# Three changes of order in a hybrid encoder layer on one core: late sums, half weight tiles, hung loads

## The chip, the cores and the metric

The kernel runs on one NeuronCore of a Trainium2 chip. Its time is the device time in microseconds of one execution. Engines of the core: PE (matrix products), DVE and ACT (element-wise work, copies out of the accumulators), POOL (here mostly an issuer of DMAs, also those that add into their target) and SP (an issuer of DMAs). Each takes its instructions in order.

## The reference

One layer of an encoder is run on a prompt of 1024 frames and a sample of 32 frames, with shared weights, in float32:

```python
h = rms_norm(x, g_pre_mix)
qa, ka, va, ra, alr, qb, kb, vb, ga, gb = split_cols(h @ w_in)
oa, s_gla = gla_branch(qa, ka, va, ra, alr, w_a2, b_a2, g_gla, gla_s0, gla_block)   # 4 heads, gated linear recurrence
ob, k_rows, v_rows = attn_fn(qb, kb, vb, rel_bias)                                  # 8 heads, band of 9 chunks of 64
mix = (sigmoid(ga) * (oa @ w_br_a) + sigmoid(gb) * (ob @ w_br_b)) @ w_out
x = x + rms_norm(mix, g_post_mix)
f, conv_new = conv_ffn(rms_norm(x, g_pre_ffn), conv_s0, w_up, conv_w, conv_b, w_down)
x = x + rms_norm(f, g_post_ffn)
gate = sigmoid(rms_norm(x, g_pre_ple) @ w_ple_gate)
x = x + rms_norm(gate * (pe @ w_ple), g_post_ple)
```

The sample's attention reads cached keys and values as well (`cache_attn_k`, `cache_attn_v`), its recurrence starts from a given state (`state_gla`). The outputs are the new x of both groups, the last keys and values, the recurrence's states and the convolution's.

## The kernel before

Prompt and sample lie side by side, T = 1056 columns; a row is a tile of 128 features by 1056 columns, 528 KB. Products in float32 are made of three passes of a rounded format: every operand is split into a high part (a copy by ACT) and a low part (the difference, by DVE), and PE multiplies high by high, high by low and low by high. So each weight tile is loaded (`raw`, two buffers), split into `whi` and `wlo`, and used.

The order of PE, DVE and ACT is the order of the program text, written out by hand from stage to stage. The order of the DMAs on SP and POOL is planned at build time: the planner places each where it expects its operands and its buffer to be ready. On the chip an issuing engine then waits, in that order, at each DMA until its operands are there, with all later ones behind it.

**Band stage (about 303 to 576 us).** Eight heads (hp 0 to 3, hd 0 and 1) of nine blocks each: eight blocks of 128 queries and one for the sample. One loop runs over all 72 blocks. For block i it makes the scores (`probs`: PE products L1039 and L1040 into the only accumulator pair `two`, then L1045 on DVE, which adds the bias and takes the row minimum), then the transposes of block i-1 (`transposed`: PE L1052, ACT's high part L1054, DVE's low part L1055 put off into `LOWS`), ACT's exponential L1046, a step of the next head's preparation (`prepare`: splits of q, k and v, copies of kh and kl to the other 64 partitions by DMAs L1001 and L1004, transposes of v), one `piece` of a filler (the products L862 to L895 of other weight tiles, whose results `fv`, four buffers, ACT evacuates in L734 and L870), and at last the output of block i-2 (`third`: PE L1093; `gather`: ACT copies half of it in L1059, DVE adds the other half to it in L1060; L1117 to L1119 for the sample). The accumulators `one` are four banks, `mm` two, `two` one pair. Before the loop, rows q, k and v of the first two heads are loaded (L1242), 18 pieces run, and the steps of the first `prepare` lie between them. Their loads are kc (L965) and cv (L967), the cached keys and values, and the bias tile of each head (L979, then two POOL memsets L980 and L981).

**Recurrence stage (about 576 to 866 us).** Four heads of four segments, u = 0 to 15. In each, level factors of segment u+1 (`X`, DVE L1361 to L1398, ACT L1377 to L1383) are made beside the products of segment u; L1451 and L1454 turn the scores, L1522 uses them. The filler goes on: `load_tile` (L790 loads half a tile, L792 a whole one), ACT L817/L820 and DVE L818/L821 split it, POOL adds finished parts into DRAM (L749) and places new operands (L777, L778). In a head's last segment the sample's state tile `ss` (one buffer) is loaded (L1539), used, updated by L1528 and stored (L1529). `sr` rows are loaded in L1544 and stored in L1599.

**Branch stage (about 866 to 992 us).** 12 products of a band row block (`branch_b`), then 28 of the other branch (`branch_a`, L1968 to L1970, about 3 us each) in a hand-written sequence `seq`; `order_w` lists their 30 half tiles of weights in order of use. `weights_load` loads two halves into one tile of `raw`, `split_weights` splits half i two products before its use (ACT L1830, DVE L1831), and with every even i asks for the pair i+2. `pair_load` (L1937) loads gate rows into buffers that POOL's adding DMAs (L1952) must have left. After this stage come the output product, the feed-forward part and the embedding part, which the change does not touch.

Of the kernel before, what the change touches and what calls it, by code (L numbers as in the profile page):

```python
# [12 lines left out]
F32 = mybir.dt.float32  # L13
# [3 lines left out]
ALU = mybir.AluOpType  # L17

P = 128
D = 1024  # L20
KT = 8
NP = 1024
NS = 32
# [22 lines left out]
LATE = 4  # L46
# [68 lines left out]
def emit(tc, a):  # L115
# [12 lines left out]
    def tl(p, shape, dt=F32, tag=None, bufs=None):  # L128
        tag = tag or nm("t")
        kw = {} if bufs is None else {"bufs": bufs}  # L130
        return p.tile(list(shape), dt, name=nm(tag), tag=tag, **kw)
# [27 lines left out]
    wp = pool("wp")  # L159
# [802 lines left out]
    def band_loads(hp):  # L962
        d = B.setdefault(hp, {})
        d["kc"] = tl(bp, [P, 512], tag="kc")
        dma.dma_start(d["kc"], a["cache_k"][hp])  # L965
        d["cv"] = tl(bp, [P, 4, P], tag="cv")
        dma.dma_start(d["cv"], a["cache_v"][hp])  # L967

    def prepare(g):
        hp, hd = divmod(g, 2)  # L970
        d = B[hp]
        r = slice(64 * hd, 64 * hd + 64)
        o = slice(64 - 64 * hd, 128 - 64 * hd)
        if hd == 0:
            band_loads(hp)
        qs, kh, kl = [tl(bp, [P, w], F32R, tag=f"{x}{hd}") for x, w in (("qs", T), ("kh", T + 512), ("kl", T + 512))]
        vs = tl(bp, [P, 13, P], F32R, tag=f"vs{hd}")
        bias = tl(bp, [P, NS + 640], tag="bias", bufs=2)
        dma.dma_start(bias, a["rel"][2 * hp + hd])  # L979
        po.memset(bias[64:128, NS : NS + 64], NEG)  # L980
        po.memset(bias[0:64, NS + 576 : NS + 640], NEG)  # L981
        d[hd] = qs, kh, kl, vs, bias
        parts = [(slice(0, HT), d["k"][:, one]), (slice(HT, T), d["k"][:, two]), (slice(T, T + 512), d["kc"])]

        def high(i):
            ac.activation(kh[r, parts[i][0]], parts[i][1][r], AF.Copy)

        def low_part(i):
            ve.tensor_tensor(kl[r, parts[i][0]], parts[i][1][r], kh[r, parts[i][0]], op=ALU.subtract)

        high(0)
        yield
        high(1)
        low_part(0)
        yield
        high(2)
        low_part(1)
        yield
        ac.activation(qs[r], d["q"][r], AF.Copy)
        low_part(2)  # L1000
        dma.dma_start(kh[o].bitcast(F32), kh[r].bitcast(F32))  # L1001
        yield
        ve.tensor_tensor(qs[o, one], d["q"][r, one], qs[r, one], op=ALU.subtract)
        dma.dma_start(kl[o].bitcast(F32), kl[r].bitcast(F32))  # L1004
        yield
        ps = ps_one()
        for j in range(8):
            pe.transpose(ps[:, 64 * j : 64 * j + 64], d["v"][r, j * P : (j + 1) * P], ident[r, r])
        src = ps.rearrange("p (j f) -> p j f", f=64)
        ac.activation(vs[:, 0:8, r], src, AF.Copy)  # L1010
        ve.tensor_tensor(qs[o, two], d["q"][r, two], qs[r, two], op=ALU.subtract)
        ve.tensor_tensor(vs[:, 0:8, o], src, vs[:, 0:8, r], op=ALU.subtract)
        yield
        ps = ps_one()
        pe.transpose(ps[:NS, :64], d["v"][r, NP:], ident[r, r])
        ac.activation(vs[:NS, 12:13, r], ps[:NS, :64].rearrange("p (j f) -> p j f", f=64), AF.Copy)
        ve.tensor_tensor(vs[:NS, 12:13, o], ps[:NS, :64].rearrange("p (j f) -> p j f", f=64), vs[:NS, 12:13, r], op=ALU.subtract)
        ac.activation(vs[:, 8:12, r], d["cv"][:, :, r], AF.Copy)
        yield
        ve.tensor_tensor(vs[:, 8:12, o], d["cv"][:, :, r], vs[:, 8:12, r], op=ALU.subtract)  # L1020
        yield

    LOWS = []

    def band_head(hp, hd):
        r = slice(64 * hd, 64 * hd + 64)
# [30 lines left out]
        def gather(ps, n, out):  # L1057
            t = tl(bp, [P, 256], tag="ot", bufs=2)[r, :n]
            ac.activation(t, ps[o, :n], AF.Copy)  # L1059
            ve.tensor_tensor(out, ps[r, :n], t, op=ALU.add)  # L1060

        def pair(t):
            use = [range(max(0, 2 * t + j - 4), 2 * t + j + 1) for j in range(2)]
# [35 lines left out]
        def sample():  # L1099
            got = {}  # L1100

            def first():
                got["s"] = probs(NP, NS, NP, 512 + NS, -NS)

            def second():
                p = got["p"] = tl(bp, [P, 10, P], F32R, tag="pt", bufs=3)
                transposed([(got["s"], NS + b * P, P) for b in range(4)], NS, [p[:, :4, x : x + NS] for x in (0, NS)])
                transposed([(got["s"], 0, NS)], NS, [p[:NS, 4:5, x : x + NS] for x in (0, NS)])

            def third():  # L1110
                vs = d[hd][3]
                ps = ps_one()
                for k in range(5):
                    n = P if k < 4 else NS
                    pe.matmul(ps[:, : 2 * NS], vs[:n, 8 + k], got["p"][:n, k, : 2 * NS], start=(k == 0), stop=(k == 4))
                t = tl(bp, [P, 256], tag="ot", bufs=2)[r, : 2 * NS]
                ac.activation(t, ps[o, : 2 * NS], AF.Copy)  # L1117
                ve.tensor_tensor(t, ps[r, : 2 * NS], t, op=ALU.add)
                ve.tensor_tensor(d["ob"][r, NP:], t[:, :NS], t[:, NS:], op=ALU.add)  # L1119

            return [(first, second, third)]

# [138 lines left out]
    for i in range(len(WORK) + SK + 1):  # L1261
        g, j = divmod(i, NW)
        hp, hd = divmod(g, 2)
        if g < 8:
            if j == 0:
                if hd == 0:
                    band_sums(hp)
                steps = prepare(g + 1) if g < 7 else decays(0)
            if j == 3 and hd == 0:
                B[hp]["ob"] = evt()  # L1270
            WORK[i][0]()
            if SK <= i:
                WORK[i - SK][1]()
            B[hp]["exp"].pop()()
            next(steps, None)
            if j % 3 == 2:
                next(made, None)
            if hd == 0 and hp < 3 and j in (5, 7) or hd and hp < 3 and j == 0:
                band_row(hp + 1, {5: 0, 7: 1, 0: 2}[j])
            if g == 7 and j in (6, 7):  # L1280
                head_value(0, j - 6)
            if j == 5 and g:
                weight_sum(*divmod(g - 1, 4), B[hp]["sums"][hd][0:1, 0:1])
            if j % 3 == 1 and g:
                n = 3 * (g - 1) + j // 3
                if n < 4 * HK:
                    branch_sum(n, B[hp]["sums"][hd][0:1, 0:1])
        piece()
        n = i - SK - 1
        if n >= 0 and WORK[n][2]:  # L1290
            WORK[n][2]()
        if len(WORK) <= i < len(WORK) + SK:
            WORK[i - SK][1]()
        for f in LOWS:
            f()
        LOWS.clear()
        flush()
        if fill["n"] < 18 + (BAND_PIECES - 18) * (i + 1) / (len(WORK) + SK + 1):
            piece()
        next(end, None)  # L1300
        if n >= 0 and n % (2 * NW) == 2 * NW - 1:
            end = band_end(n // (2 * NW))
            next(end)
# [230 lines left out]
    def loads(u):  # L1534
        g, h, s, t0, nt = seg(u)
        r = R.setdefault(u, {})
        if nt > 256:
            r["ss"] = tl(gp, [P, 256], tag="ss")
            dma.dma_start(r["ss"], a["state_gla"][h])  # L1539

    def gates(u):
# [286 lines left out]
    def branch_half(key, t):  # L1828
        h, l = wsp[key] = [tl(wp, [P, HK, P], F32R, tag=x, bufs=4) for x in ("whi", "wlo")]
        ac.activation(h, t, AF.Copy)  # L1830
        ve.tensor_tensor(l, t, h, op=ALU.subtract)  # L1831
# [3 lines left out]
    def weight_of(n, m):  # L1835
        if n == "b":
            return a["w_br_b"][3, :, HK * (m % 2) : HK * (m % 2) + HK].rearrange("p k c -> p (k c)")
        if n[0] == "a":
            return branch_quarter(int(n[1]) - 1, int(n[2]) - 1, m)
        return d_wa[m, :, ("s0", "s1", "s3", "s2").index(n)]  # L1840

    def weights_load(i):
        if i < len(order_w) and order_w[i] not in raws:
            raw = tl(wp, [P, KT, P], tag="raw", bufs=2)
            for j, u in enumerate(order_w[i : i + 2]):
                raws[u] = raw[:, HK * j : HK * j + HK]
                dma.dma_start(raws[u].rearrange("p k c -> p (k c)"), weight_of(*u))

    for n in (4, 5, 6):
        dma.dma_start(gb[n] if n < 6 else oa[KT - 1][0].bitcast(F32), d_gb[n])  # L1850
# [181 lines left out]
        at.setdefault(use[u] - 2, []).append(u)  # L2032

    def split_weights(u):
        i = order_w.index(u)
        if i % 2 == 0:
            weights_load(i + 2)
        branch_half(u, raws.pop(u))

    weights_load(0)  # L2040
    work = {0: [(first_sum, 0), (first_split, 0)], 1: [(first_sum, 1), (first_split, 1)], 2: [(first_sum, 2), (first_split, 2)],
            3: [(first_sum, 3), (first_split, 3)], 4: [(t1_split, 0), (t1_split, 1)], 5: [(t1_split, 2), (t1_split, 3)], 6: [(t2_sum, 0), (t2_sum, 1)],
            7: [(t2_split, 0), (t2_sum, 2)], 8: [(t2_split, 1), (t2_sum, 3)], 9: [(t2_split, 2), (t2_split, 3)], 10: [(third_sum, 0)], 11: [(b22_split, 0)],
# [1264 lines left out]
```

## Time and profile before

| | us |
|---|---|
| median of 3 runs | 1864.64 |
| lowest, highest | 1861.52, 1873.78 |
| the profiled execution | 1872.21 |
| its span | 1870.5 |
| PE busy in it | 1826.9 |

The profile's numbers are of the profiled execution, its span a little shorter than its time. A row of the timeline gives start, duration, engine, line, operation, the tile written and those read, the shape, and in brackets the idle time of the engine before it and what ended that. A row of the waits gives total, times and longest. A row of a stretch of time gives its length, the busy time of PE, PEld (weight loads), DVE, ACT and POOL, then TensorE's mean granted clock (1.00 is full), the busy share of the DMA engines and GB/s. SPq is SP's queue of DMAs.

### The profile page before, as it was taken

The page shows a single profiled execution, that of the slowest core. Times are in us where ns is not written, and L with a number is a line of the kernel's source. Part 1 is how long each engine was busy: PE and PEld are TensorE (multiplying, and loading weights), DVE is VectorE, ACT ScalarE, POOL GpSimd, SP SyncE. Part 2 cuts the span into 40 slices and gives each one's busy share as a digit, 9 for nine tenths or more (in the row PEclk, how much of TensorE's full clock was granted, in tenths as well). Part 3 has the DMA queues.
Part 4 walks back from the last instruction along what each step waited for, and adds up shares of the span by engine and source line. Part 5 has one row for each costly group of instructions (what it writes and reads, how often), then busy time and mean ns, then how long its engine had stood idle before and what let it go on. Part 6 is the DMA issues. An engine that isn't in the chain of part 4 may idle for free.

```text
span 1870.5 us, 36262 instructions
## 1 busy us (share of the span) xinstructions
PE 1826.9 (98%) x14000; PEld 1789.8 (96%) x14000; DVE 1298.1 (69%) x2451; ACT 1005.0 (54%) x2126; POOL 351.9 (19%) x609
## 2 busy tenths in 40 slices
PE   8999999999999999999999999999999999999996
PEld 8999998899999998998999999999999999999996
DVE  6955542666656875877847776888888875568776
ACT  7544233666667776766636555433333345555555
POOL 0043441132201121110010121122223211000102
PEclk9999999999999999999999999999999999999998
DMA  7278986778667889877595477676878779887746
GB/s 284 84 223 244 273 220 204 193 209 244 193 176 240 263 258 226 225 182 269 190 250 174 159 266 279 198 229 211 243 210 224 177 216 307 294 267 250 237 136 111
DMA packets 171449, 413.24 MB, mean 221 GB/s; under 512 B 21956, under 2 KB 56972, under 8 KB 170380
## 3 DMA queue, kind: packets, MB, share of 16 engines
q1 hardware_dynamic: 116156, 252.99, 40.7%
q0 software_dynamic: 53680, 153.24, 32.5%
q10 hardware_dynamic: 1440, 4.69, 0.6%
q8 instruction: 110, 1.80, 0.4%
q14 instruction: 63, 0.52, 0.1%
HBM read 270.68 MB, written 181.97 MB: 242 GB/s over the span
## 4 chain that ended last, share of the span: by engine, by line
PE 82%; DMA 6%; DVE 5%; ACT 5%; issue 2%; POOL 0%; SPq 0%; ACTq 0%; DVEq 0%; POOLq 0%
PE two L2533 6%; PE two L2531 6%; PE two L2532 6%; PE mm L228 3%; PE mm L226 3%; PE mm L227 3%; PE two L2980 3%; PE two L2982 3%; PE two L2981 3%; PE two L641 3%; PE two L642 3%; PE two L643 3%; PE mm L893 3%; PE mm L862 3%; PE mm L863 2%; PE mm L895 2%
## 5 line engine op out<-in xcount | busy, mean ns | idle before, releaser
L2982 PE MATMUL two<-d,wlo 128*128 128x264 f32 x616 | 174.3, 283 | 0.8 <-DVE wlo L2716 0.8
L2981 PE MATMUL two<-d,whi 128*128 128x264 f32 x616 | 174.7, 284 | 0.2 <-DVE d L2667 0.2
L2980 PE MATMUL two<-d,whi 128*128 128x264 f32 x616 | 174.6, 284 | 0.0
L2521 ACT ACTIVATE whi<-ws 128x512 fp32r<-128x512 f32 x88 | 55.5, 632 | 161.8 <-PE two L2532 154.5
L862 PE MATMUL mm<-xh,whi 128*128 128x264 f32 x448 | 135.7, 303 | 2.2 <-ACT fv L870 2.1
L863 PE MATMUL mm<-xl,whi 128*128 128x264 f32 x448 | 128.0, 286 | 0.0
L864 PE MATMUL mm<-xh,wlo 128*128 128x264 f32 x448 | 127.6, 285 | 0.0
L2532 PE MATMUL two<-ml,whi 128*128 128x264 f32 x448 | 126.4, 283 | 0.0
L2533 PE MATMUL two<-mh,wlo 128*128 128x264 f32 x448 | 126.0, 284 | 0.0
L2531 PE MATMUL two<-mh,whi 128*128 128x264 f32 x448 | 125.8, 283 | 0.0
L2982 PEld LDWEIGHTS two<-d,wlo 128*128 128x128 f32 x616 | 116.4, 189 | 1.1 <-DVE wlo L2716 1.0
L2981 PEld LDWEIGHTS two<-d,whi 128*128 128x128 f32 x616 | 115.8, 188 | 0.4 <-DVE d L2667 0.4
L2980 PEld LDWEIGHTS two<-d,whi 128*128 128x128 f32 x616 | 115.7, 188 | 0.0
L893 PE MATMUL mm<-xh,whi 128*128 128x352 f32 x312 | 109.6, 351 | 3.4 <-ACT fv L734 3.4
L895 PE MATMUL mm<-xh,wlo 128*128 128x352 f32 x312 | 101.9, 327 | 0.0
L894 PE MATMUL mm<-xl,whi 128*128 128x352 f32 x312 | 101.7, 326 | 0.0
L642 PE MATMUL two<-tl,whi 128*128 128x264 f32 x320 | 90.7, 284 | 0.0
L641 PE MATMUL two<-th,whi 128*128 128x264 f32 x320 | 90.7, 283 | 0.0
L643 PE MATMUL two<-th,wlo 128*128 128x264 f32 x320 | 90.7, 284 | 0.0
L862 PEld LDWEIGHTS mm<-xh,whi 128*128 128x128 f32 x448 | 85.5, 191 | 4.2 <-ACT fv L870 3.5
L2716 DVE TENSOR_TENSOR wlo<-wraw,whi 128x512 fp32r<-128x512 f32 (+1 forms) x81 | 51.7, 644 | 50.9 <-ACT whi L2715 50.8
L863 PEld LDWEIGHTS mm<-xl,whi 128*128 128x128 f32 x448 | 85.1, 190 | 0.0
(802 smaller groups left out, 6854.3 us busy)
## 6 DMA issues: line engine op xcount, KB each, us to landing
raw<-in_w_in SPq DMA_DIRECT2D x36, 512.0 KB, 4.6
d_b<-av POOLq DMA_DIRECT2D x33, 528.0 KB, 4.5
d_ws<-in_w_down POOLq DMA_DIRECT2D x24, 704.0 KB, 8.3
uraw<-d_b SPq DMA_DIRECT2D x32, 528.0 KB, 5.4
raw<-in_w_up SPq DMA_DIRECT2D x29, 512.0 KB, 4.1
d_gs<-in_w_in POOLq DMA_DIRECT2D x48, 256.0 KB, 6.2
sraw<-in_w_up SPq DMA_DIRECT2D x22, 512.0 KB, 5.1
wraw<-d_ws SPq DMA_DIRECT2D x16, 704.0 KB, 5.8
```

Source lines behind the costliest of these rows:

```text
L641: pe.matmul(ps[:, j, :HC], w[0][:, k], x[0](k, s), start=st, stop=False, skip_group_check=True)
L642: pe.matmul(ps[:, j, :HC], w[0][:, k], x[1](k, s), start=False, stop=False, skip_group_check=True)
L643: pe.matmul(ps[:, j, :HC], w[1][:, k], x[0](k, s), start=False, stop=sp_, skip_group_check=True)
L862: pe.matmul(ps, h[:, k], xh[:, b, s], start=(k == 0 and not (half and x.chain)), stop=False, skip_group_check=True)
L863: pe.matmul(ps, h[:, k], xl[:, b, s], start=False, stop=False, skip_group_check=True)
L893: pe.matmul(ps, wh, h[:, k, s], start=(k == 0), stop=False)
L2531: pe.matmul(ps[:, j, :HC], w[0][:, k], x[0][:, k, s], start=st, stop=False, skip_group_check=True)
L2532: pe.matmul(ps[:, j, :HC], w[0][:, k], x[1][:, k, s], start=False, stop=False, skip_group_check=True)
L2533: pe.matmul(ps[:, j, :HC], w[1][:, k], x[0][:, k, s], start=False, stop=sp_, skip_group_check=True)
L2980: pe.matmul(o, wh, xh_[:, s], start=(k == 0 and p in (0, 4, 5)), stop=False, skip_group_check=True)
L2981: pe.matmul(o, wh, xl_[:, s], start=False, stop=False, skip_group_check=True)
L2982: pe.matmul(o, wl, xh_[:, s], start=False, stop=(k == HD - 1 and p in (3, 4, 6)), skip_group_check=True)
```

## The change

Three things change, and no product, split or transfer of data is added or left out.

1. The sum of a block's output (L1060; for the sample L1118 and L1119) is put into a list `LATE`, which the loop empties after the next block's scores (and, at the end of a pair of heads and after the last block, at the end of the iteration).
2. The branch's weights: two `raw` tiles are kept for the whole stage as four half slots. At the start the first four halves are loaded; after half i is split, half i+4 is loaded into its slot.
3. Three kinds of loads are hung on values: before cv of hp 0, before the bias tiles of hp 0 and before each `ss`, POOL writes one element (4 bytes, 7 DMAs in all) into the tile that is to be loaded, taken from the row v, from kh of the first head, or from the factors `X` of the segment. The load overwrites it and so must follow it.

```diff
         d["cv"] = tl(bp, [P, 4, P], tag="cv")
+        if hp == 0:
+            po.dma_start(d["cv"][0:1, 0, 0:1], d["v"][0:1, 0:1])
         dma.dma_start(d["cv"], a["cache_v"][hp])
...
         bias = tl(bp, [P, NS + 640], tag="bias", bufs=2)
+        if hp == 0:
+            po.dma_start(bias[0:1, 0:1], B[0][0][1][0:1, 0:1].bitcast(F32) if hd else d["v"][0:1, 0:1])
         dma.dma_start(bias, a["rel"][2 * hp + hd])
...
-    LOWS = []
+    LOWS, LATE = [], []
+
+    def late_sums():
+        for f in LATE:
+            f()
+        LATE.clear()
...
             ac.activation(t, ps[o, :n], AF.Copy)
-            ve.tensor_tensor(out, ps[r, :n], t, op=ALU.add)
+            LATE.append(lambda: ve.tensor_tensor(out, ps[r, :n], t, op=ALU.add))
...
-                ve.tensor_tensor(t, ps[r, : 2 * NS], t, op=ALU.add)
-                ve.tensor_tensor(d["ob"][r, NP:], t[:, :NS], t[:, NS:], op=ALU.add)
+
+                def sums():
+                    ve.tensor_tensor(t, ps[r, : 2 * NS], t, op=ALU.add)
+                    ve.tensor_tensor(d["ob"][r, NP:], t[:, :NS], t[:, NS:], op=ALU.add)
+
+                LATE.append(sums)
...
             WORK[i][0]()
+            late_sums()
             if SK <= i:
...
+        if i >= len(WORK) or n >= 0 and n % (2 * NW) == 2 * NW - 1:
+            late_sums()
         next(end, None)
...
             r["ss"] = tl(gp, [P, 256], tag="ss")
+            po.dma_start(r["ss"][0:1, 0:1], X[u][0:1, 0, 0:1])
             dma.dma_start(r["ss"], a["state_gla"][h])
...
     def weights_load(i):
-        if i < len(order_w) and order_w[i] not in raws:
-            raw = tl(wp, [P, KT, P], tag="raw", bufs=2)
-            for j, u in enumerate(order_w[i : i + 2]):
-                raws[u] = raw[:, HK * j : HK * j + HK]
-                dma.dma_start(raws[u].rearrange("p k c -> p (k c)"), weight_of(*u))
+        if i < len(order_w):
+            if i in (0, 2):
+                raws[i] = tl(wp, [P, KT, P], tag="raw", bufs=2)
+            t = raws[order_w[i]] = raws[i & 2][:, i % 2 * HK : i % 2 * HK + HK]
+            dma.dma_start(t.rearrange("p k c -> p (k c)"), weight_of(*order_w[i]))
...
     def split_weights(u):
-        i = order_w.index(u)
-        if i % 2 == 0:
-            weights_load(i + 2)
         branch_half(u, raws.pop(u))
-
-    weights_load(0)
+        weights_load(order_w.index(u) + 4)
+
+    for i in range(4):
+        weights_load(i)
```

## The prediction

> **What bounds the kernel now.** I read the page's head first, then the waits of PE, then stretches of the span with their granted clock.
>
> ```profile
> span 1870.5 us, 36262 instructions
> PE 1826.9 (98%) x14000; PEld 1789.8 (96%) x14000; DVE 1298.1 (69%) x2451; ACT 1005.0 (54%) x2126; POOL 351.9 (19%) x609
> PE 82%; DMA 6%; DVE 5%; ACT 5%; issue 2%; POOL 0%; SPq 0%; ACTq 0%; DVEq 0%; POOLq 0%
> ```
>
> The reader is to see that PE bounds the whole: 1870.5 - 1826.9 = 43.6 us of idle PE is all that an edit of order can win, and the change adds or takes no matmul. The chain's fourth line gives PE 82% and DMA 6%: where PE stood, a transfer often ended the wait.
>
> ```profile
> PE one L1522 <- DVE turned L1454: 4.2, 1, 4.2
> PE mm L893 <- ACT fv L734: 3.4, 1, 3.4
> PE two L1039 <- DVE sm L1045: 3.2, 4, 1.0
> PE two L1968 <- ACT half L1977: 1.8, 1, 1.8
> PE two L1968 <- ACT ev L840: 1.1, 1, 1.1
> ```
>
> These are the waits that the change can reach (total, times, longest): 13.7 us in eight gaps. The granted clock adds to two of them:
>
> ```profile
> 303.00:320.00 17.00, 14.01 (x71) 13.00 (x72) 6.15 (x12) 7.20 (x16) 0.00 (x0) 0.80 0.54 155
> 734.00:751.00 17.00, 12.76 (x75) 12.08 (x75) 6.59 (x19) 13.01 (x38) 1.72 (x2) 0.80 0.92 229
> 944.00:958.00 14.00, 12.20 (x100) 11.99 (x99) 3.84 (x6) 4.10 (x9) 0.86 (x1) 1.00 1.05 309
> ```
>
> The third number from the end is the mean granted clock. Behind the gaps of 3.4 and 4.2 us it is 0.80 over 17 us, so 17 x 0.20 = 3.4 us of PE work is lost at each. Around the gap of 1.8 us (third row) it is 1.00. A gap over some 3 us therefore costs itself and 3.4 us more.
>
> **The change, part by part.**
>
> *The three hung loads, first place (cv and the two bias tiles).* They now follow a 4-byte POOL DMA that waits for the row v (one of the bias tiles: for kh).
>
> ```profile
> 289.44 0.45 SPq L967 DMA_DIRECT2D cv<-in_cache_v  x1
> 289.99 1.74 SPq L979 DMA_DIRECT2D bias<-in_rel  x2
> 291.83 1.68 SPq L1242 DMA_DIRECT2D ev<-d_b  x3
> ...
> 304.42 1.18 ACT L986 ACTIVATE kh<-ev 64x528 fp32r<-64x528 f32 x2 [9.14 <-DMA ev<-d_b]
> 305.50 0.44 ACT L734 ACTIVATE fv<-mm 128x352 f32<-128x352 f32 x1
> ...
> bias<-in_rel SPq DMA_DIRECT2D x2, 336.0 KB, 11.1
> cv<-in_cache_v SPq DMA_DIRECT2D x1, 256.0 KB
> ...
> 290.00:297.00 7.00, 7.00 (x45) 7.00 (x44) 0.00 (x0) 0.93 (x2) 5.97 (x26) 1.00 0.95 247
> 297.00:303.00 6.00, 5.55 (x35) 5.26 (x33) 0.00 (x0) 0.00 (x0) 0.58 (x4) 1.00 1.00 393
> ```
>
> The loads of q, k and v are issued at 291.83, behind cv and two bias tiles: 256 + 2 x 336 = 928 KB that nobody needs yet. ACT stands 9.14 us for k, and the evacuation L734 that frees PE's bank stands behind ACT's two L986. In that stretch the DMA engines are full (share 1.00) at 393 GB/s. 928 KB at 393 GB/s are 2.4 us; at the 247 GB/s of the 7 us before 3.8. I take 2.8. L986 then starts at 301.6, L734 ends at 303.2, and PE's gap falls from 3.4 to 0.6: **2.8 us**. With a gap of 0.6 the half clock goes too: **3.4 us**.
>
> What is late next: cv and bias themselves. Their price is that of a POOL gate and a load begun late:
>
> ```profile
> L599 POOL DMA_DIRECT2D d_gs<-c x32: 497/528/1190, 95.6 to 277.5; - x32
> DMA to landing us min/median/max: 1.5/3.4/5.5
> ...
> L979 SPq DMA_DIRECT2D bias<-in_rel x8: 327/332/1147, 290.0 to 504.1; - x8
> DMA to landing us min/median/max: 2.9/3.2/11.1
> ...
> 317.94 0.22 PE L1039 MATMUL two<-kh,qs 128*128 128x128 f32 x1
> 321.06 0.28 PE L1039 MATMUL two<-kh,qs 128*128 128x256 f32 x1
> ```
>
> L599 is the nearest row, a 4-byte gate DMA of the kernel as it is. v is 528 KB behind k, 1.4 us at 393 GB/s, so it lands by 303.0. Two gates (0.5 us each on POOL), 3.4 us to landing, SP's issue, 3.2 us to landing and two memsets of 0.15 us bring bias to 303.0 + 1.1 + 3.4 + 0.4 + 3.2 + 0.3 = 311.4. The first scores move from 317.94 to 317.94 - 6.2 = 311.7, and PE needs their sum L1045 only for the second ones, 3.1 us later. So it costs nothing, with some 2.5 us in hand. With the longest landings (5.5 and 11.1) bias comes at 321.4 and PE stands about 7 us: both ends are kept. Behind the hung loads on SP stand stores of fv (four buffers), the copies of kh and kl (L1001, L1004) and a weight load; on POOL only the bias memsets. I charge 0.5 us for that.
>
> [...]
>
> *The hung loads, second place (ss, four heads).*
>
> ```profile
> SPq L1539 <- DMA out_o_gs<-ss: 3.2, 1, 3.2
> 723.07 0.68 DVE L821 TENSOR_TENSOR wlo<-raw,whi 128x512 fp32r<-128x512 f32 x1
> 727.75 0.87 SPq L790 DMA_DIRECT2D raw<-d_gs  x2
> 737.25 0.63 ACT L820 ACTIVATE whi<-raw 128x512 fp32r<-128x512 f32 x1 [5.83 <-DMA raw<-d_gs]
> ```
>
> The weight tile is free at 723.75 (L821's end), but its load goes out at 727.75: SP stands 3.2 us at the next head's state load, which waits for the store of the last state out of the same single buffer and is needed only four segments later. ACT, free since 731.4, waits 5.83 us for these weights, and PE's 4.2 us follow. Without ss ahead the load goes out at about 724.0, 3.75 us earlier, and with the same transfer time lands as much earlier: the gap falls to 4.2 - 3.75 = 0.45. **3.8 us, and 3.4 us** of clock. The new ss load hangs on the factors of its own segment, behind a gate on POOL whose neighbours are the adds L749; they have four buffers of slack, so I take 0, with the end at a full return of the stall (a rival below).
>
> *Band's sums one block later.* L1060 (and half of the sample's L1118) stand behind the next block's L1045 on DVE instead of ahead of L1055.
>
> ```profile
> DVE ev L1060 <- ACT ot L1059: 59.4, 30, 3.8
> 453.11 1.08 ACT L999 ACTIVATE qs<-ev 64x1056 fp32r<-64x1056 f32 x1
> 454.87 0.38 ACT L1059 ACTIVATE ot<-one 64x256 f32<-64x256 f32 x1
> 455.29 0.42 DVE L1060 TENSOR_TENSOR ev<-one,ot 64x256 f32<-64x256 f32 x1 [2.88 <-ACT ot L1059]
> 456.69 0.81 DVE L1045 CUSTOM_DVE_ANT_0 s<-two,bias 128x640 f32<-128x640 f32 x1
> 327.16 0.68 DVE L939 TENSOR_TENSOR wa<-s,wa 16x512 fp32r<-16x512 f32 x1 [2.92 <-ACT wa L937]
> 329.56 0.41 PE L1039 MATMUL two<-kh,qs 128*128 128x320 f32 x1 [0.65 <-DVE sm L1045]
> ```
>
> DVE stands 59.4 us at this sum, but that is nearly all free: PE pays only where L1045 comes late, the 3.2 us of four L1039. At 455 the chain is plain: ACT's long L999 makes L1059 late, L1060 waits 2.88 us, and L1055, a low part and L1045 queue behind it. The first of the four gaps (329.56, 0.65) has L939 with its 2.92 us before it and no L1060; it stays. The other three, 3.2 - 0.65 = **2.6 us**, go: without the wait L1045 starts about 1.1 us earlier, which covers the longest gap of 1.0. No instruction is added; each sum holds its bank of four and its buffer of two half a block longer, and the 0.42 us of L1060 now lies ahead of preparation work that has whole blocks of slack: 0. Were that cover gone, 31 x 0.42 = 13 us would be the price.
>
> *Branch weights by halves.* The two halves of a tile were already separate loads; now each is issued when its own half is split, four products ahead.
>
> ```profile
> 941.34 0.68 DVE L1831 TENSOR_TENSOR wlo<-raw,whi 128x512 fp32r<-128x512 f32 x1
> 945.84 0.40 SPq L1847 DMA_DIRECT2D raw<-d_wa  x1
> 955.16 0.63 ACT L1830 ACTIVATE whi<-raw 128x512 fp32r<-128x512 f32 x1 [5.80 <-DMA raw<-d_wa]
> ```
>
> The load at 945.84 waited for both halves; its first half was free at 942.02. Issued 3.8 us earlier it covers most of ACT's 5.80 and all of PE's 1.8. The gap of 1.1 has the same shape. Together **2.9 us**. SP still carries the loads of the gate rows, which wait for additions of POOL and hold what is behind them, and 512 KB more go out at the stage's start: at 393 GB/s 1.3 us, beside weights that are wanted several products later. Bounds 0 to 2.9; I take 2.7.
>
> **The sum.** 2.8 + 3.4 + 3.8 + 3.4 + 2.6 + 2.7 - 0.5 = 18.2 us. The profiled execution took 1872.2 us (1.7 of it around the span), so 1854.0. That execution is 7.6 us above the median of the other runs, 1864.6, which go from 1861.5 to 1873.8. Two half clocks are 6.8 us; I read the median as a run that lacks them and so has 18.2 - 6.8 = 11.4 us to lose, which gives 1853.2. **Forecast 1854.**
>
> **The rivals.**
>
> *The wait moves (1861).* A gate or the bias load lands as late as its rows allow, and PE stands at the second scores in place of k. A gap of 3.5 us with its half clock costs 6.9: 1854 + 6.9 = 1861. For it: bias has taken 11.1 us; the queue is full there. Against: most landings were 3.2.
>
> [...]
>
> *SP is held at the hung loads (1869, slower).* A state load now waits for a POOL gate, and the weight loads behind it in SP's order are as late as at 727.75. If SP stands 3.5 us or more at two of the four heads, the gain of 7.2 is gone and one such stall is added: 1854 + 7.2 + 7.6 = 1869. Below some 3 us of standing ACT's wait doesn't reach PE, which is the point that decides. For it: where a load goes in SP's queue is planned, not written. Against: it needs POOL to be late twice, and POOL is busy 19%.
>
> *It doesn't do what it says (1861).* SP's planned order still has a store's wait ahead of the weights at 727: 1854 + 7.2 = 1861.
>
> *The median has it all (1846).* If the slow profiled run had other reasons, the median loses the whole 18.2: 1846.4.
>
> **How the numbers follow.** Forecast 0.57 (its own range 1848 to 1859), wait moves 0.12, held 0.08, not as said 0.08, all of it 0.15. The range 1845 to 1865 leaves the held case and the tails out. One per cent, 18.6 us, is about what a measurement of this kernel can tell from no change: under 1846.0 counts as faster (half of the last case and the forecast's tail: 0.10), above 1883.3 as slower (0.03), the rest 0.87.
>
> **What would show it.** PE's idle time at L893 near 303 under 1 us and no stretch of clock under 1.00 between 300 and 800; cv and bias issued after the rows; the weight load L790 of the third head's start within 0.5 us of its tile's release; L1039 waiting once, near 329; ACT L1830 waiting under 2 us for raw. Wrong would make it: a PE gap at L1039 near 312 to 316 that ends on bias, or SP standing at L967, L979 or L1539 with a weight load behind it.

## The result, and the profile after

The changed kernel takes 1854.25 us (median of 20 runs, 1851.5 to 1861.85) beside 1865.59 for the kernel before in the same comparison (20 runs, 1860.62 to 1873.78): the ratio is 0.9942, with a 95% interval of 0.9931 to 0.9952. In a repeat it was 1854.03 beside 1865.79, ratio 0.9939 (0.9922 to 0.9956). The profiled execution took 1853.27 us. One of the twelve runs of the kernel before in its own repeat took 10134.89 us and enters none of the means below.

The lines below come from the head of the page after, then from the waits of PE (total, times, longest).

```profile
span 1851.6 us, 36353 instructions
PE 1818.7 (98%) x14000; PEld 1784.1 (96%) x14000; DVE 1301.8 (70%) x2451; ACT 1003.1 (54%) x2126; POOL 356.4 (19%) x616
```

```profile
PE mm L862 <- ACT fv L870: 2.7, 6, 0.8
PE mm L471 <- ACT z L454: 1.7, 1, 1.7
...
PE two L1048 <- DVE sm L1054: 0.7, 1, 0.7
```

Idle PE is 1851.6 - 1818.7 = 32.9 us, 10.7 less than the 43.6 before. Of the five waits that the prediction listed only one is left: L1048, which was L1039, waits once instead of four times. The waits for L734, turned, half and ev are gone. (Lines after the first edit are numbered 2 to 17 higher than in the kernel before; the experiments lie in between.)

The three stretches of time again, the first two with their clock (third number from the end):

```profile
303.00:320.00 17.00, 17.00 (x108) 16.12 (x107) 7.46 (x17) 8.99 (x21) 1.67 (x7) 1.00 0.68 198
734.00:751.00 17.00, 16.59 (x127) 15.98 (x126) 12.60 (x39) 11.69 (x40) 2.75 (x4) 1.00 0.87 240
944.00:958.00 14.00, 14.00 (x118) 14.00 (x117) 6.01 (x10) 6.16 (x12) 1.72 (x2) 1.00 0.87 245
```

PE is busy without a break around 303 and 950, and the clock is 1.00 where it was 0.80. The timeline around 303 shows how:

```profile
300.21 1.19 ACT L990 ACTIVATE kh<-ev 64x528 fp32r<-64x528 f32 x2 [4.84 <-DMA ev<-d_b]
301.30 0.44 ACT L734 ACTIVATE fv<-mm 128x352 f32<-128x352 f32 x1
301.99 0.57 POOL L968 DMA_DIRECT2D cv<-ev  x1 [6.43 <-DMA ev<-d_b]
302.54 0.52 POOL L982 DMA_DIRECT2D bias<-ev  x1
...
304.11 0.34 SPq L969 DMA_DIRECT2D cv<-in_cache_v  x1
304.65 0.33 SPq L983 DMA_DIRECT2D bias<-in_rel  x1
305.08 0.53 SPq L1005 DMA_DIRECT2D kh<-kh  x1
305.71 0.54 SPq L1008 DMA_DIRECT2D kl<-kl  x1
...
308.11 0.15 POOL L984 MEMSET bias<- 64x64 f32 x1 [4.56 <-DMA bias<-in_rel]
...
311.46 0.22 PE L1048 MATMUL two<-kh,qs 128*128 128x128 f32 x1
```

The gate of cv goes out as v lands, cv and the first bias follow at 304, and bias is ready at 308.4 (the second memset's end), 3 us before the first scores at 311.5, to which it is added.

The result has two halves, and the mean granted clock, which every run lists, separates them. The profiles of before and after end at half clock with no product running: the mean clock is 0.62 over the last 13.5 us of the one and 0.59 over the last 13.6 us of the other. A run's time multiplied by one minus its clock, less 6.0 us for that tail (what is left in the runs of the changed kernel; its second profile, 1852.0 us at a clock of 0.997, loses 5.6 us in all), is what half clocks cost it, and time multiplied by clock is its length at full clock. The tail costs 5.1 us in the profile of before (13.5 x 0.38) and 5.6 us in the one after (13.6 x 0.41), and the first profile of the changed kernel does lose 1.7 us near 34 us; so the 0 of the changed kernel is where the count starts, not a proof that nothing is lost. The last two columns are means over the runs of a kernel (6 to 12; 19 to 35 of the kernel before), and the standard error of a difference between two kernels is 0.5 to 1.0 us; a run's clock is listed in steps of 0.001, which is 1.9 us of its time. The last row is a control: the same kernel against itself.

| kernel | median | kernel before, same chip | ratio (95%) | at full clock, against before | lost to half clocks (before) |
|---|---|---|---|---|---|
| the change, again | 1854.0 | 1865.8 | 0.9939 (0.9922 to 0.9956) | -8.7 | 0 (2.9) |
| band's loads alone | 1866.4 | 1865.2 | 1.0009 (0.9997 to 1.0022) | +0.7 | 3.7 (2.3) |
| state's loads alone | 1864.4 | 1865.2 | 0.9994 (0.9978 to 1.0009) | -0.2 | 1.5 (2.3) |
| late sums alone | 1863.3 | 1865.2 | 0.9990 (0.9975 to 1.0005) | -3.8 | 3.6 (2.3) |
| half tiles alone | 1862.6 | 1865.2 | 0.9991 (0.9978 to 1.0003) | -1.6 | 2.1 (2.3) |
| all but band's loads | 1857.0 | 1865.5 | 0.9953 (0.9936 to 0.9969) | -8.3 | 1.7 (2.7) |
| all but state's loads | 1859.4 | 1865.5 | 0.9962 (0.9946 to 0.9978) | -6.7 | 2.1 (2.7) |
| all but late sums | 1860.3 | 1865.5 | 0.9974 (0.9964 to 0.9985) | -3.1 | 0.8 (2.7) |
| all but half tiles | 1857.1 | 1865.5 | 0.9957 (0.9940 to 0.9974) | -7.2 | 1.4 (2.7) |
| sums and tiles only | 1859.5 | 1865.8 | 0.9970 (0.9956 to 0.9984) | -6.7 | 3.2 (2.9) |
| sums behind the low parts | 1856.8 | 1865.8 | 0.9950 (0.9933 to 0.9967) | -6.6 | 0 (2.9) |
| the kernel before, again | 1864.4 | 1865.8 | 0.9992 (0.9979 to 1.0005) | -1.0 | 2.0 (2.9) |

So of the 11 us, 8 to 9 are work (7.7 by the first runs of the changed kernel) and 2 to 3 are half clocks that no longer happen.

### The profile page after: what moved, and what is told of

Read it like the earlier page. It is cut to its first block, busy times and chain, and to the rows that moved or that the text cites. A ratio compares the mean times of both kernels' runs of the same rounds, so it can differ in the third digit from the quotient of the medians.

```text
span 1851.6 us, 36353 instructions
## 1 busy us (share of the span) xinstructions
PE 1818.7 (98%) x14000; PEld 1784.1 (96%) x14000; DVE 1301.8 (70%) x2451; ACT 1003.1 (54%) x2126; POOL 356.4 (19%) x616
## 5 line engine op out<-in xcount | busy, mean ns | idle before, releaser
L862 PE MATMUL mm<-xh,whi 128*128 128x264 f32 x448 | 135.1, 302 | 2.8 <-ACT fv L870 2.7
L893 PE MATMUL mm<-xh,whi 128*128 128x352 f32 x312 | 108.5, 348 | 0.0
L862 PEld LDWEIGHTS mm<-xh,whi 128*128 128x128 f32 x448 | 84.9, 190 | 4.7 <-ACT fv L870 4.2
```

Of the source, the lines that this page charges most:

```text
L862: pe.matmul(ps, h[:, k], xh[:, b, s], start=(k == 0 and not (half and x.chain)), stop=False, skip_group_check=True)
L893: pe.matmul(ps, wh, h[:, k, s], start=(k == 0), stop=False)
```

## The experiments

**One part alone.** Four kernels, each the kernel before with one of the edits shown in the change. First the hung v cache and bias:

```diff
+        if hp == 0:
+            po.dma_start(d["cv"][0:1, 0, 0:1], d["v"][0:1, 0:1])
...
+        if hp == 0:
+            po.dma_start(bias[0:1, 0:1], ...)
```

> The kernel before with one part of the change alone: the band's v cache and bias hang on values of their users. My theory (each part's gain is its own gap and the clock lost behind it): PE's idle gap of 3.4 us near 303 and the half clock behind it at 307 to 314 are gone, the profiled run is 6.2 us shorter at that place (2.8 and 3.4), and the median falls by 3 us (the gap alone, if most runs have no half clock there) to 6 us: 1859 to 1862 beside 1865 before. Rival, only the half clock counts: the gap goes and the median falls by under 1 us. Rival, the planner's new order of transfers downstream does it: the gap near 303 stays or the gain appears elsewhere.

Measured: 1866.35, no gain. From the waits of PE of this kernel:

```profile
PE mm L862 <- ACT fv L870: 5.3, 6, 3.1
...
PE two L1044 <- DMA kl<-kl: 1.6, 1, 1.6
```

The wait at L893 near 303 is gone as predicted, but a new one of 1.6 us stands at the first low product of the scores, nine microseconds later. It ends on the copy of kl to the other partitions (L1008). That copy is no later than before (issued at 307.0, before at 307.8); PE reaches it 5.7 us sooner, at 312.2 in place of 317.9. Behind it 3.4 us go by at half clock (the mean is 0.57 from 315 to 319, and 2 x 4 x 0.43 = 3.4). My theory fell: the gap goes, and about half of it comes back at the next late transfer. The rival "only the half clock" wasn't put to the test, since half clocks were not fewer (3.7 us beside 2.3). The third rival gets a part: a gap of 3.1 us near 709 (in the row of L862) is new beside the first profile of before. The chain that ends last there starts at a store of `sr`; SP stands behind it at the next load of `sr`, and the weights L790 are late: ACT waits 5.0 us for them.

Next the state's load:

```diff
+            po.dma_start(r["ss"][0:1, 0:1], X[u][0:1, 0, 0:1])
             dma.dma_start(r["ss"], a["state_gla"][h])
```

> The kernel before with one part alone: the state load of each head hangs on a value, so that SP isn't held at it. My theory: the gap of 3.8 us near 729 and the half clock at 737 to 744 are gone, 7 us in a profiled run that has both, of which some 2 may be given back at 729 to 755 by small gaps as the changed kernel does; the median falls by 2 to 5 us. Rival, only the half clock counts: under 1 us. Rival, the new order of transfers does it: the gap near 729 stays and the gain is elsewhere, in the feed-forward stage.

Measured: 1864.37, no difference that can be told. SP's queue of the kernel before, then of this one:

```profile
723.57 0.42 SPq L1529 DMA_DIRECT2D out_o_gs<-ss  x1
727.30 0.35 SPq L1539 DMA_DIRECT2D ss<-in_state_gla  x1
727.75 0.87 SPq L790 DMA_DIRECT2D raw<-d_gs  x2
```

```profile
720.41 0.42 SPq L1529 DMA_DIRECT2D out_o_gs<-ss  x1
720.93 0.91 SPq L790 DMA_DIRECT2D raw<-d_gs  x2
```

The weights now go out 0.5 us behind the store instead of 4.2: SP's part is as predicted. The profile's gap at 734 is not there either, but that proves nothing, for it is also missing in three profiles in which the state is loaded as before (half tiles alone and, below, all but state's loads, and sums and tiles only), and the time at full clock falls by 0.2 us. The two profiles of before (the last experiment has the second) show longer executions than its average run, and this gap belongs to them.

Third, the late sums:

```diff
-            ve.tensor_tensor(out, ps[r, :n], t, op=ALU.add)
+            LATE.append(lambda: ve.tensor_tensor(out, ps[r, :n], t, op=ALU.add))
...
             WORK[i][0]()
+            late_sums()
```

> The kernel before with the band's output sums one block later, nothing else. The prediction's sum gives 2.6 us (three of four gaps at the sums). What the two traces show by matmul number gives 4.8 us, since the gaps at the next matmuls behind it, which the prediction kept, go too. Rival, the part seen above 2.6 belongs to the hung loads: 2.6 or less here, and the rest in the kernel with the band's loads alone. The gaps near 303 and 729 stay as they were.

Measured: 1863.29. At full clock 3.8 us are won, between the two sizes, and 1.3 us more than before are lost to half clocks. The other gaps did not stay as expected: 1.9 us near 303, none at 734, and one of 4.0 us at L862 from 707 on, where the first profile of before has none over 0.8. As with the band's loads alone, SP stands there at the load of `sr` behind a store that takes 8.7 us; in the kernel with half tiles alone that store takes 3.6 us, and no gap follows.

Fourth, the half tiles:

```diff
+            t = raws[order_w[i]] = raws[i & 2][:, i % 2 * HK : i % 2 * HK + HK]
...
+        weights_load(order_w.index(u) + 4)
```

> The kernel before with the branch's weights by half tiles, four products ahead, nothing else. The prediction's sum gives 2.7 us and the two traces 3.2 us, both at the first product of the branch stage, whose waits for weights go. Rival, that gain comes from the earlier stages' loads being hung, not from the half tiles: 0 to 0.5 us here. Rival, the new order of transfers costs in the feed-forward stage what it wins: 0 in the median with the branch's gaps gone.

Measured: 1862.55, 1.6 us at full clock; the profile has none of the two waits L1968. The rival that this gain belongs to the hung loads falls; the size is six tenths of the predicted one.

**One part left out.** The changed kernel without one part, in the same order:

```diff
-            po.dma_start(d["cv"][0:1, 0, 0:1], d["v"][0:1, 0:1])
-            po.dma_start(bias[0:1, 0:1], ...)
```

> The changed kernel without its hung v cache and bias (the other three parts stay). In the parts alone, time multiplied by granted clock (what the run would take at full clock) fell by 3.7 us with the late sums and 1.6 us with the half tiles, and not at all with the hung loads of the band (up by 0.7) or of the state (down by 0.2); the whole change gives 7.7. If parts simply add up, the band's loads are worth nothing and this run takes as long as the changed kernel, 1854 to 1855. If they win only in the company of the others, it is 2 to 4 us slower, 1856 to 1858, with a gap of 1.3 to 3.5 us at the first product near 303 in its profile.

Measured: 1856.95. The median and the gap of 3.0 us at 303 are those of the second reading; at full clock the kernel is as long as the changed one (-8.3 beside -8.7; the 7.7 above is that of the changed kernel's first runs), as the first has it. No half clock stands behind the gap:

```profile
PE mm L893 <- ACT fv L734: 3.0, 1, 3.0
```

```profile
303.00:320.00 17.00, 13.98 (x90) 13.16 (x89) 7.88 (x16) 8.94 (x21) 0.53 (x1) 1.00 0.63 185
```

By these means the band's loads win no work that can be told from none (0.4 us with an error of 1); more of their 3 us of median (1857.0 beside 1854.0, on two chips) is clock, 1.7 us lost beside none.

```diff
-            po.dma_start(r["ss"][0:1, 0:1], X[u][0:1, 0, 0:1])
```

> The changed kernel with the state loaded as before. If parts add up, as long as the changed kernel. If it is the state's load that holds SP in front of the gate weights, whatever else is done, 2 to 4 us slower with an idle gap of 3 us or more of PE at 705 to 735. If the gap of the kernel before there is an accident of the transfers in flight (the kernels with the band's loads or the late sums alone have it near 709, that with half tiles alone not at all), the profile shows it in no fixed place and the mean lies 1 to 2 us up.

Measured: 1859.41 over 8 runs that spread from 1853.6 to 1862.6. The profiled execution is one of the short ones and has no gap there: the store goes out at 710.98, the state at 713.97, the weights at 714.42, and nothing waits for them. Neither reading holds whole. The median is 5.4 us up and the mean 4.3, more than either gave; 2.0 us of that are work and 2.1 clock. The second wanted the gap, which this profile doesn't have, but a short execution can't show what makes the long ones long. What it does show is that SP's stand (2.5 us of waiting) doesn't have to reach PE.

```diff
-            LATE.append(lambda: ve.tensor_tensor(out, ps[r, :n], t, op=ALU.add))
+            ve.tensor_tensor(out, ps[r, :n], t, op=ALU.add)
```

> The changed kernel with the band's sums as before. If parts add up: 3.7 us slower, 1858, with the waits for sm back (four gaps of 0.6 to 1.1 us). The prediction's sum makes it 2.6 us slower. If the sums won only by shifting what comes behind, under 1 us.

Measured: 1860.30, the largest loss of the four, 5.6 us at full clock (8.7 - 3.1). The waits are back, and the copy of kl too:

```profile
PE two L1043 <- DVE sm L1049: 3.3, 4, 1.0
...
PE two L1044 <- DMA kl<-kl: 1.7, 1, 1.7
```

```diff
-        weights_load(order_w.index(u) + 4)
+        if i % 2 == 0:
+            weights_load(i + 2)
```

> The changed kernel with the branch's weights loaded by whole tiles. If parts add up: 1.6 us slower, with PE's gaps of about 1.1 and 1.8 us at the branch's first products back. The prediction's sum makes it 2.7 us slower. If the early loads being hung had already brought these weights in time, none.

Measured: 1857.08; 1.5 us at full clock, the same as alone. One of the two gaps is back (L1985, 1.3 us).

**Pairs and repeats.** Sums and tiles together, without any hung load:

```diff
-            po.dma_start(...)   # cv, bias, ss
```

> The kernel before with late sums and half tiles; both sets of loads are issued as before. If parts simply add up: the 5.3 us of full-clock time that the two parts showed alone, 1859 to 1860 in the median. If the hung loads matter only together (the changed kernel without either of them was within 1.5 us of it at full clock, so each covers for the other): the same 5 us. If sums and tiles together already give all: 1854 to 1856, and the loads are worth nothing.

Measured: 1859.45, 6.7 us at full clock: 77% of the work that the whole change wins. The first reading comes nearest; the 5.4 of the two parts alone and this agree within their error. The hung loads add 2.0 us of work and all of the clock: this kernel loses 3.2 us to half clocks, as much as the kernel before.

The changed kernel with the sum right behind the low parts of its own block:

```diff
         LOWS.clear()
+        late_sums()
         flush()
...
             WORK[i][0]()
-            late_sums()
```

> The changed kernel with the band's output sum put right behind the low parts of the same block, so still ahead of the next block's scores on DVE. If the sum costs because DVE stands at it for ACT's copy with the low parts behind it, this is as fast as the changed kernel, 1854 to 1855, and waits at the scores for sm stay below 0.7 us. If what counts is that the next block's sm comes before the sum (0.3 us of DVE work and its wait), it loses most of the 4 us that the sums give: 1857 to 1859, with gaps of 0.6 to 1.1 us for sm back.

Measured: 1856.82, 2.1 us more at full clock than the changed kernel. Both readings are half right. DVE's idle time at the sum (row of its line in this kernel) and PE's wait:

```profile
  ACT ot L1068: 24.7, 16
```

```profile
PE two L1048 <- DVE sm L1054: 1.9, 4, 0.7
```

DVE stood 59.4 us at the sum before, 24.7 here, and 0.4 in the changed kernel. Passing the low parts brings about six tenths of the sum's gain (3.5 of 5.6 us at full clock, the kernel with the sums as before being the start), passing the next scores the rest.

The changed kernel and the kernel before, once more on the chip of these runs:

> The changed kernel once more, on the chip of these runs: 1854 in the median, 11 us below the kernel before; in its profile no gap over 1 us at 303 and none over 1.7 us at 700 to 740. A gap for the copy of kl near 312 of up to 1.1 us is possible, as in the kernels of one part less.

Measured: 1854.03. No gap near 303 and none over 1 us from 700 to 740; but the copy of kl holds PE, and longer than the 1.1 us expected:

```profile
PE two L1049 <- DMA kl<-kl: 1.4, 1, 1.4
```

> The kernel before once more, for a second profile: 1865 in the median. If the gaps of 3.4 us at 303 and 4.2 us at 734 belong to the program's order, they are there again in the same places within 0.5 us. If their size is set by the transfers that happen to be in flight, as kernels with the same loads there suggest (1.3, 1.9 and 1.7 us at 303; at 734 nothing, with 3.1 and 4.0 us near 709 instead), the second profile has other sizes or places, and a shorter time than the first profile's 1872.

Measured: 1864.38. The profiled execution took 1871.9 us, and its other runs 1861.2 to 1865.4, but for the one of 10134.89. From the waits of PE and the stretches of its profile:

```profile
PE one L1522 <- DVE turned L1454: 4.2, 1, 4.2
PE mm L862 <- ACT fv L870: 3.3, 5, 1.5
PE two L1039 <- DVE sm L1045: 3.2, 4, 1.0
PE mm L893 <- ACT fv L734: 2.4, 1, 2.4
```

```profile
303.00:320.00 17.00, 14.59 (x75) 13.29 (x74) 6.15 (x12) 6.23 (x13) 0.00 (x0) 0.80 0.63 187
734.00:751.00 17.00, 12.81 (x80) 11.96 (x80) 5.57 (x17) 11.47 (x35) 1.63 (x2) 0.80 0.95 244
```

The four waits at the scores are the same to a tenth; the gap at 303 is 2.4 instead of 3.4, the one at 734 is there again (its start 2.2 us later), and the two waits of the branch stage are missing altogether. Both profiled executions of the kernel before have both half clocks and both end near 1872, 7 us above its median. Both theories get a part. The gap at 303 is 1.3 to 3.4 us long in the seven profiles whose band loads are as before and at most 0.5 us in the seven whose loads are hung: the program's order makes it, and its size varies. The gap at 734 is in two of the seven profiles whose state is loaded as before, so the order alone doesn't make it.

No version tried beat the changed kernel.

## Why the prediction was right, and where it was not

The forecast was 1854.0 with 18.2 us off the profiled execution and 11.4 off the median; measured were 18.9 and 11.3. The sizes of several steps were off, and their errors cancelled; that both totals came out within 1 us is luck, the kinds of gain were not. Two pairs of profiles (before and after; both again) can be laid over each other by the number of the matmul; the start of the same matmul then says how much is won between two points.

| step | predicted | first pair | second pair |
|---|---|---|---|
| band's loads, gap and clock | 2.8 + 3.4 | 6.4 | 3.6 |
| late sums | 2.6 | 4.7 | 4.7 |
| state's loads, gap and clock | 3.8 + 3.4 | 7.8, then 2.7 given back | 8.4, then 1.4 given back |
| half tiles | 2.7 | 2.9 | 1.5 |

In the second pair 2.0 us more lie ahead of 100 us, where the change has no part. Which gain belongs to which part, two pairs can't say, since all parts change at once. All fourteen profiles can: each is laid over the first profile of before, and the table gives the time by which it is shorter in a stretch, as range and mean of the profiles with the part and of those without (sums behind the low parts left out of the second row; there it is 2.8). With six to eight profiles on a side and the other parts mixed, a mean is good to about 1 us.

| part, stretch (products that start there in before) | with the part | without it | difference |
|---|---|---|---|
| band's loads, 300 to 320 us | 3.5 to 6.4, 4.9 | 0 to 5.0, 2.9 | 2.0 |
| late sums, 320 to 576 us | 4.1 to 4.8, 4.6 | -1.6 to 0.1, -0.7 | 5.2 |
| state's loads, 700 to 800 us | 5.0 to 6.4, 5.6 | -0.6 to 6.1, 3.1 | 2.5 |
| half tiles, 866 to 1100 us | 1.1 to 3.2, 2.4 | -0.6 to 2.0, 1.0 | 1.4 |

The differences add up to 11.1 us, clock included, near what the median lost. The two profiles of before, which are long executions, weigh in this: without them the first and the third difference are 1.1 us each. Only the late sums separate the profiles cleanly. Band's and state's loads take away the bad executions; the good ones were as short without them.

*Band's loads.* The mechanism held in the profile: k came 4.2 us sooner (L990 starts at 300.21, L986 at 304.42) where I took 2.8, L893 no longer waits, the half clock is gone, bias was ready at 308.4 where I had 311.4. The step that failed is "what is late next: cv and bias themselves". What is late next is the copy of kl, which I had only listed among what stands behind the hung loads and charged with 0.5 us: 1.1 to 1.7 us in five of the seven profiles with these loads hung, 0.5 in one, and none in the first of the changed kernel. The rival "the wait moves" was right in kind and wrong in its place and price: not bias, and 1.1 to 1.7 us of gap instead of 3.5.

*The gate.* From L599 I took 3.4 us to landing. The rows of the new gates, band first, then state:

```profile
L982 POOL DMA_DIRECT2D bias<-kh x1: 508/508/508, 303.1 to 303.1; - x1
DMA to landing us min/median/max: 1.7/1.9/2.1
...
L1555 POOL DMA_DIRECT2D ss<-x x4: 532/540/545, 616.8 to 824.6; - x4
DMA to landing us min/median/max: 2.9/4.6/6.7
```

The same 4 bytes took 1.7 to 2.1 us in one place and up to 6.7 in another.

*State's loads.* The gap at 734 and its clock went, but the step described is only half of why. SP does stand at the hung load, and longer at the next buffer (from SP's waits between 600 and 760, after):

```profile
SPq L1561 <- DMA d_oa<-sr: 43.5, 7, 10.8
...
SPq L1556 <- DMA ss<-x: 9.6, 3, 5.0
```

The rival "SP is held" put its deciding point at some 3 us of standing. SP stood 5.0 us at once there, with weight loads behind it, which the prediction had named as a sign of being wrong, and PE had no gap: the point was too low. What was given back comes from the line above it: SP stood 10.8 us at the load of sr behind a store, the next weights went out at 734.65, and ACT waited 2.0 us for them, with small gaps of PE from 729 to 755 behind it. The prediction had nothing for what is late next in this place. Its list was wrong in two details as well: the weight load L790 went out 1.5 us behind its tile's release (712.23 and 713.71), not 0.5, and ACT waited up to 3.0 us for half tiles in the branch stage, not under 2, which PE did not feel. I had also kept the transfer time of the two late weight loads L790: in the execution profiled before, and in the kernel with the state's loads alone, they took

```profile
DMA to landing us min/median/max: 9.5/10.2/10.9
```

```profile
DMA to landing us min/median/max: 5.6/5.6/5.6
```

so the gap of 4.2 was late issue and slow transfer together. The step that failed is "with the same transfer time": in the five other kernels that load the state as before, the weights go out 3.3 to 4.7 us behind the store, as late as in before (4.2), but land 4.3 to 6.1 us after their issue instead of 9.5 to 10.9, and there is no gap at this place. The second profile of before has the slow transfer (9.6 to 11.0) and the gap. What slows the transfer is open; so is why the same store of `sr` takes 3.6 us in one execution (half tiles alone) and 8.1 and 8.7 in others (before, late sums alone).

*Late sums.* The term was mis-sized, 2.6 for 4.7. The three gaps went and the first (now at 322.7) stayed, as I said. But I counted the waits of PE's products; the weight loads ahead of them wait too, and a product whose weights come late starts late even where PE's bar shows no hole. From the waits of PEld between 320 and 576, before and after:

```profile
PEld two L1039 <- DVE sm L1045: 4.6, 5, 1.3
PEld one L1052 <- ACT s L1046: 4.2, 10, 0.6
```

```profile
PEld one L1061 <- ACT s L1055: 3.3, 8, 1.0
...
PEld two L1048 <- DVE sm L1054: 0.8, 1, 0.8
```

8.8 us before and 4.1 after: 4.7 less, the size that the matmul starts show; the waits of PE's products in the same stretch fall by only 2.2 (6.3 to 4.1). This part's waits at L1039 repeat to a tenth in the second profile of before, and it is the largest in the runs: 3.8 us alone, 5.6 in company. The two differ by no more than their errors allow; the starts give 4.1 to 4.8 in every profile that has it, alone or not.

*Half tiles.* 2.7 predicted, 1.5 to 1.6 in the runs. The two gaps of 1.8 and 1.1 us come and go: of the six profiles without half tiles two have both, two have one, and two (the second of before among them) have neither; none of the eight with half tiles has either. A single profile showed me the most that there is to win.

*The median.* I read it as a run without the two half clocks. The runs of before lose 2.3 to 2.9 us to half clocks, so an average run has less than one of the two (3.4 each), and at full clock it is about 1.6 us (second profile) and 3 to 4 us (first) shorter than the profiled ones. So the 11.4 us that I left to the median came out right as a number, made up otherwise: 8 to 9 us of work, about half of it from the sums, and 2 to 3 us of clock, of which I had counted none. That single parts win little in the median while the whole wins 11 us has two sides. The clock loss stays at 1.5 to 3.7 us with one part alone, since other gaps are left standing. And the work of the four alone adds up to 4.9 us and not to 8.7; where the other 3.8 come from no run separates. The state's loads are an example: 0.2 us of work alone and 2.0 in company, two numbers that are barely further apart than their error.

## What to carry to other kernels

Read the waits of the weight loads beside those of the products: a hole in the matmul queue can hide in the former. Before a wait is counted as a gain, look up which transfer is due next behind it, a copy within the core too, and count only the distance to that. And take a second profile, or the clock that each run lists, before gaps that end on a transfer are summed at their size in one execution: here the waits for DVE's sums repeated to a tenth of a microsecond, those on DMAs varied from none to 4 us. Better still, lay all profiles at hand over each other by the number of the product: a part that wins in every one is then told from a part that only takes away bad executions.

## What was unexpected of the hardware

In these profiles the price of a PE gap in clock doesn't follow from its length. The prediction had "a gap over some 3 us costs 3.4 us more, one of 1.8 nothing". The rows, by kernel: the stretch behind the same wait L471 of 1.69 us before and after, then the gap of 1.9 us at 303 in the kernel with late sums alone, then the one of 3.1 us near 709 in the kernel with the band's loads alone.

```profile
34.00:39.00 5.00, 4.04 (x31) 3.83 (x32) 5.00 (x6) 4.14 (x9) 0.00 (x0) 1.00 0.48 193
```

```profile
34.00:39.00 5.00, 4.39 (x23) 4.39 (x24) 5.00 (x6) 4.14 (x8) 0.00 (x0) 0.66 0.51 203
```

```profile
303.00:320.00 17.00, 15.09 (x78) 13.80 (x77) 6.15 (x12) 7.24 (x16) 0.00 (x0) 0.80 0.63 194
```

```profile
709.00:717.00 8.00, 4.93 (x35) 4.59 (x35) 5.99 (x19) 5.54 (x23) 1.73 (x2) 1.00 1.09 350
```

The same 1.69 us cost no clock in one execution and 1.7 us (5 x 0.34) in another; 1.9 us cost 3.4 (17 x 0.20), 3.1 us cost none, and 3.0 us at 303 none in the kernel without the band's loads. (Lost clock isn't always lost time: the product behind the wait starts at 34.52 us in the first row's execution and at 34.61 in the second's, and ten microseconds on, at 44.72 and 44.81, the second is still only 0.1 us behind.)

It doesn't seem to take even one such gap. In the kernel with the band's loads alone the mean clock is 0.57 from 328.5 to 332.5 us, with PE busy throughout, 14 us after its wait for kl ended (at 314.07); its waits for DVE's sums are 0.9 us at the longest:

```profile
328.50:332.50 4.00, 4.00 (x17) 3.58 (x16) 2.68 (x6) 3.08 (x6) 0.00 (x0) 0.57 0.91 252
```

The same happens in the kernel with late sums alone (0.59 from 331 to 335) and in the one with half tiles alone (0.57 from 331.5 to 335.5, its waits for the sums 1.1 us at the longest). The kernel before has gaps of 0.65 and 1.05 us for the sums at 329.56 and 333.63, and its clock is 1.00 from 330 to 338, as it is from 328 to 338 in the changed kernel without late sums. From 737.3 to 744.1 in the kernel before the mean clock is 0.50, half of full. By the length and mean clock of the rows, stretches at half clock last 6.8 us (2 x 17 x 0.20) or 3.4 (2 x 5 x 0.34). What decides between the executions is open.
